# Eight Strassen steps in eight units of a hybrid decoder block, with halves joined and biases added by accumulating transfers

## The chip, the cores and the metric

The kernel runs on one core of a Trainium2 chip. The metric is the device time of one execution in microseconds (us); lower is better. "Before" and "after" name the kernel without and with the change.

## The reference

One layer of a decoder block over 256 tokens of width 4096, in float32. Everything large in it is a product of a 256-row activation with a weight matrix:

```
h      = rmsnorm(x, norm_w)                                # 256 x 4096
proj   = h @ w_in                                          # 4096 x 20480
u_p, z_p, u_c, b_c, c_c, z_c (2048 each), g_logit (8192) = split(proj)
y_pool = (pooled(u_p) @ pool_w, four groups) * pool_scale * silu(z_p)
y_conv = b_c * conv3(c_c * u_c) * silu(z_c)                # causal, width 3
br     = y_pool @ w_branch[0], y_conv @ w_branch[1]        # 2048 x 4096 each
merged = sum over n of sigmoid(g_logit[n] + gate_b[n]) * br[n]
out    = rmsnorm(x + merged @ w_out, final_norm_w)         # 4096 x 4096
```

## The kernel before

**Units and steps.** The work is cut into units of 1024 output columns: for the product with `w_in` the units cu, cc, cz, cb (convolution branch, two of each), pz, pu (pooling branch, two of each) and g0_0 to g1_3 (gates, two branches by four column blocks); for `w_branch` b0_0 to b1_3; for `w_out` o0 to o3. A unit goes through its contraction dimension in steps of 256 rows: 16 steps, in the branch units 8. A step loads one block of 256 x 1024 weights (1 MB) on SyncE's queue into one of three buffers (`raw`).

**Precision by splitting.** An operand is kept as a high part rounded to TensorE's float32r and a low part that holds the rest. Each product is three matmuls: high by high, high by low, low by high. ScalarE makes the high part (line 69), VectorE subtracts to make the low part (line 72). The split weights go into `ring`, a circular store of 60 pieces of 1 KB a partition; preparation runs at most three steps ahead of the multiplication (`AHEAD`) and stops when the ring is full.

**Two kinds of step.** A P step is 2 x 2 x 2 plain block products of 128 x 128 by 128 x 512: 24 matmuls, and two copies and two subtractions of 1024 columns to prepare it; it takes 16 pieces of the ring. An S step is one level of Strassen's scheme (the variant with shared sums): seven block products, 21 matmuls, and in preparation sums of weight blocks as well (`V`, `raw`), with three copies and three subtractions; it takes 28 pieces. For an S step the stationary operand, 128-column blocks of the activation, needs four sums besides its own four blocks (Q3, Q5, Q6, Q7). There is room for these in seven of the 16 operands of a unit (`NS_X = 7`, the operands at 9 to 15); the other nine (`NP_X = 9`) can only be used in P steps. Which steps of a unit are S is written out by the functions `sequence`, `late_sequence` and `spread_sequence` (lines 539 to 572).

**End of a unit.** The products of S steps accumulate in two sets of PSUM banks. One set (`sums`) is evacuated by ScalarE into `E`, the other (`shared`) is joined into `R` (or `Y` in cu1) by `joins`, on ScalarE and VectorE. Then `combine` (line 447) has VectorE add E to R: in one piece of 2048 columns, or in two of 1024 where the unit has `halves` set (gates and outputs). What follows for the unit, its `epi`, is a list of small operations and empty places; `tick` (line 1110) takes one entry for every six matmuls of the next unit. A gate's list is

```python
return gap(1) + halves(lambda t: add(R[:, t], R[:, t], Y[:, 0])) + gap(3) + [
    lambda: act(R, R, AF.Sigmoid), lambda: move(gates_d[n, c], R)]
```

where `Y[:, 0]` holds the bias, loaded three quarters into the unit. An output unit's list loads x into E, adds it to R in two halves after ten empty places, takes the squares on ScalarE, multiplies by the final norm's weights (Y) and stores R (line 753).

**Order.** All instructions are kept in program order on their engine. A transfer written as `move` is issued by GpSimd's queue, `load` by SyncE's. GpSimd runs ahead of the others until something it must wait for holds it, and it then holds whatever stands behind it. From g1_3 on, operands of the branch units, and later of the output units, are fetched from memory by `move` into `sa` (and into `sb` beside it) and filled in by ScalarE and VectorE as their places become free (`pop_fill`, line 838); a fill is put at least six ticks behind its fetch.

**Memory of a partition.** `R`, `E` and `Y` are 8 KB each for the whole kernel. `Y` holds the product of the convolution and pooling branches, from g0_0 on the biases, then the gate that a branch unit needs, and final norm weights.

Of the kernel before, what the change touches and what calls it, by code (L numbers as in the profile page):

```python
# [56 lines left out]
def hybrid_block(ctx: ExitStack, tc: tile.TileContext, x, x_t, norm_t, w_first, w_in, pool_w, pool_scale,  # L57
# [34 lines left out]


# [13 lines left out]
    Y = sb("Y", [P, 2, NU])  # L107
# [19 lines left out]
    m_d = dram.tile([4, P, 4, 2, T], F32, name="m_d")  # L127
    z_d = dram.tile([2, P, 2, NU], F32, name="z_d")
    o_d = dram.tile([3, P, 2, NU], F32, name="o_d")

# [16 lines left out]


    place = {}

    def replace_by(name):
        if place:
            place["stack"].close()
        place["stack"] = stack = ExitStack()
        ctx.enter_context(stack)
        return stack.enter_context(tc.tile_pool(name=name, bufs=1))
# [24 lines left out]
    class Operand:  # L181


        def __init__(self, kind, view, region):
            self.kind, self.view, self.region = kind, view, region
            self.ready = False

# [39 lines left out]
    class Step:  # L227
# [95 lines left out]
        def groups(self):  # L323
# [14 lines left out]
            elif self.kind == "P":  # L338
                order = [(t, n) for n in self.halves for t in self.toks]
                if self.ending:  # L340
                    order = [(t, n) for t in self.toks for n in self.halves]
                for t, n in order:
                    mm = []
                    for k in range(2):
                        ah, al = self.op.standing(k, t)
                        h, l = self.h[n][:, k], self.l[n][:, k]
                        mm += [(ah, h), (ah, l), (al, h)]
                    gs.append([("E", t, n), mm, None])
                    if self.final and t == self.toks[-1]:
                        gs[-1][2] = [(self.blocks[n], 8)]  # L350
            elif self.kind == "S":
                prods = {"M1": (A11, self.dh, self.dl, 0, ("F", 0, 0)),
                         "N3": (Q3, self.dh, self.dl, 1, ("E", 0, 0)),
                         "M2": (A12, self.dh, self.dl, 2, ("E", 0, 1)),
                         "N5": (Q5, self.h13, self.l13, 0, ("F", 0, 1)),
                         "N7": (Q7, self.h13, self.l13, 1, ("F", 1, 0)),
                         "N6": (Q6, self.h24, self.l24, 0, ("F", 1, 1)),
                         "N4": (A22, self.h24, self.l24, 1, ("E", 1, 1))}
                order = ("N3", "M2", "N4", "M1", "N5", "N7", "N6") if self.closing else (
                    "M1", "N3", "M2", "N5", "N7", "N6", "N4")  # L360
                v = self.op.view
                left = {}
                for nm in order:
                    o, h, l, i, bank = prods[nm]
                    mm = [(v[:, 0, o], h[:, i]), (v[:, 0, o], l[:, i]), (v[:, 1, o], h[:, i])]
# [190 lines left out]
    few = NS_X - NB  # L556

# [77 lines left out]
    def make_bands(c):  # L635
        if c == 0:
            pool = replace_by("bands")
            place.update(bands=pool.tile([P, 2, T], F32R, name="bands"), edge=pool.tile([P, 2, P], F32R, name="edge"))
            for t in range(16):
                pin(nc.gpsimd.memset(ic[:, t:t + 1], 1.0 / (t + 1)))  # L640
        bands, edge = place["bands"], place["edge"]
# [21 lines left out]
    def band_sums(st):  # L663
        c = st.band
        for b in range(8):
# [3 lines left out]
            bands, edge = place["bands"], place["edge"]  # L669
# [73 lines left out]
    def out_unit(c):  # L743
# [5 lines left out]
        def epi(u):  # L749
# [3 lines left out]
            return [lambda: move(E, xrows[:, :, cs])] + gap(10) + halves(lambda t: add(R[:, t], R[:, t], E[:, t])) + gap(3) + [  # L753
# [4 lines left out]
        seq = seq_even if c else seq_late  # L758
        if c == 3:

            seq = spread_sequence(NS_X, 1, TAIL)
# [256 lines left out]

    def before(i, fn, *args):
# [156 lines left out]
    def run_step(u, st):  # L1176
# [12 lines left out]
        while not st.op.ready:  # L1189
            pop_fill(True)  # L1190
        gs = st.groups()
# [10 lines left out]
    for u in units:  # L1202
# [4 lines left out]
        if u is last_x:  # L1207
            stages.append(replace_by("more").tile([P, 4, P], F32, name="sb"))
# [3 lines left out]
        for st in u.steps:  # L1212
# [6 lines left out]
            pump()  # L1219
            if u.before and st is u.steps[len(u.steps) * 3 // 4]:  # L1220
# [153 lines left out]
```

## Time and profile before

| | us |
|---|---|
| median of 3 runs | 2393.96 (2393.4 to 2394.25) |
| the profiled execution | 2393.45 |
| its span, first to last instruction | 2391.7 |
| mean granted TensorE clock | 0.999 of full speed |
| VectorE busy | 2101.4 |
| ScalarE busy | 1351.9 |

Times in a profile are us from the start of the span unless marked ns. PE is TensorE's matmul, PEld its load of the stationary operand, DVE is VectorE, ACT ScalarE, POOL GpSimd and SP SyncE. In a group, `out<-in` gives the program's names for what is written and read, then the shape, `xcount`, and behind the bar the busy time, the mean length in ns of one, and behind the next bar how long the engine sat idle just before these instructions and what ended most of that time. In a row of a timeline stand the start, the length, the engine, the line and the instruction, and in brackets the idle time before it. L69 is the helper for ScalarE, L72 the one for two-operand operations of VectorE, L91 that for a transfer of GpSimd's queue, L1122 the matmul of P and S steps.

### The profile page before, as it was taken

Reading aid. Unit: us, or ns where it says so; the run is one execution under the profiler, and the core shown is the slowest. Engines: PE = TensorE matmul, PEld = TensorE weight load, DVE = VectorE, ACT = ScalarE, POOL = GpSimd, SP = SyncE. Lnnn points to the kernel's source line nnn. Section 1 sums busy time; section 2 is a strip of 40 time slices with the busy share of each in tenths; the row PEclk is TensorE's granted clock in tenths of the full one; section 3 lists DMA queues with packets and bytes.
Section 4 is the critical chain, followed back from the end, with each engine's and each line's share of the span. In section 5 each row is a group of like instructions: output and inputs, shape, how many; then the busy total and the mean of one; then the engine's idle time right before and its main releaser. Section 6 shows DMA issues by size and latency. Waiting matters only on the chain.

```text
span 2391.7 us, 27786 instructions
## 1 busy us (share of the span) xinstructions
PE 2379.3 (99%) x10604; PEld 1971.1 (82%) x10604; DVE 2101.4 (88%) x2095; ACT 1351.9 (57%) x1392; POOL 60.6 (3%) x134
## 2 busy tenths in 40 slices
PE   9999999999999999999999999999999999999998
PEld 7888888888888888888888888888888888888886
DVE  8889999888989868968999899889888786799998
ACT  7555555555546555556555556555665555556554
POOL 0000000000000000000000000000000001000000
PEclk9999999999999999999999999999999999999999
DMA  8455565555566455546666556566766668556657
GB/s 335 172 198 198 220 232 208 201 207 194 216 242 229 184 181 224 220 176 221 236 237 229 219 216 225 209 244 236 264 241 234 223 251 290 201 214 247 251 211 273
DMA packets 79942, 538.73 MB, mean 225 GB/s; under 512 B 9280, under 2 KB 9280, under 8 KB 18624
## 3 DMA queue, kind: packets, MB, share of 16 engines
q1 hardware_dynamic: 68384, 484.51, 54.3%
q0 software_dynamic: 10992, 51.39, 6.5%
q8 instruction: 83, 1.36, 0.2%
q10 hardware_dynamic: 432, 1.07, 0.1%
q14 instruction: 51, 0.42, 0.1%
HBM read 511.75 MB, written 25.17 MB: 224 GB/s over the span
## 4 chain that ended last, share of the span: by engine, by line
PE 99%; DVE 0%; DMA 0%; ACT 0%; issue 0%; DVEq 0%; SPq 0%; ACTq 0%
PE sums L1122 79%; PE shared L1122 19%; PE shared L691 1%; PE shared L467 1%; DMA R<-in_x_t_dram 0%; PE shared L670 0%; PE shared L671 0%; PE shared L673 0%; PE shared L672 0%; DVE raw L1308 0%; DVE E L84 0%; ACT V L69 0%; ACT arena L69 0%; DVE raw L1304 0%; PE shared L972 0%
## 5 line engine op out<-in xcount | busy, mean ns | idle before, releaser
L1122 PE MATMUL sums<-ring,arena 128*128 128x512 f32 x8292 | 1941.7, 390 | 0.3 <-ACT arena L69 0.3
L1122 PEld LDWEIGHTS sums<-ring,arena 128*128 128x128 f32 x8292 | 1554.5, 188 | 322.5 <-ACT ring L69 1.2
L69 ACT ACTIVATE ring<-raw 128x1024 fp32r<-128x1024 f32 (+2 forms) x901 | 988.5, 1136 | 736.3 <-PE sums L1122 264.0
L72 DVE TENSOR_TENSOR ring<-raw,ring 128x1024 fp32r<-128x1024 f32 (+2 forms) x901 | 1162.0, 1321 | 216.3 <-ACT ring L69 184.2
L1122 PE MATMUL shared<-ring,arena 128*128 128x512 f32 x1968 | 497.2, 389 | 0.0
L1122 PEld LDWEIGHTS shared<-ring,arena 128*128 128x128 f32 x1968 | 369.4, 188 | 76.6
L69 ACT ACTIVATE ring<-V 128x1024 fp32r<-128x1024 f32 x164 | 173.2, 1056 | 109.4 <-DVE V L72 75.3
L72 DVE TENSOR_TENSOR V<-raw 128x1024 f32<-128x1024 f32 x164 | 199.7, 1217 | 0.6 <-DMA raw<-in_w_out_dram 0.5
L72 DVE TENSOR_TENSOR ring<-V,ring 128x1024 fp32r<-128x1024 f32 x164 | 199.8, 1218 | 0.3 <-ACT ring L69 0.2
L72 DVE TENSOR_TENSOR raw<-raw 128x512 f32<-128x512 f32 x164 | 113.5, 692 | 5.7
L72 DVE TENSOR_TENSOR raw<-V,raw 128x512 f32<-128x512 f32 x164 | 113.3, 691 | 5.0
L72 DVE TENSOR_TENSOR R<-R,E 128x1024 f32<-128x1024 f32 (+1 forms) x55 | 95.0, 1744 | 1.9 <-DMA E<-gates_d 1.0
L69 ACT ACTIVATE E<-sums,rin 128x512 f32<-128x512 f32 (+1 forms) x57 | 44.8, 828 | 34.9 <-PE sums L1122 34.6
L72 DVE TENSOR_TENSOR R<-R,shared 128x512 f32<-128x512 f32 x84 | 57.3, 682 | 1.1
L69 ACT ACTIVATE arena<-sa 128x512 fp32r<-128x512 f32 (+2 forms) x45 | 24.9, 572 | 53.9 <-DVE sa L72 49.0
L72 DVE TENSOR_TENSOR R<-R,Y 128x1024 f32<-128x1024 f32 (+1 forms) x28 | 40.3, 1446 | 0.0
L72 DVE TENSOR_TENSOR arena<-sa,arena 128x512 fp32r<-128x512 f32 (+2 forms) x45 | 27.2, 621 | 11.7 <-ACT arena L69 11.7
L69 ACT ACTIVATE R<-R 128x2048 f32<-128x2048 f32 x8 | 15.3, 1911 | 14.5 <-DVE R L72 14.5
L467 PEld LDWEIGHTS shared<-ident,R 128*128 128x128 f32 x160 | 19.4, 140 | 4.2
L467 PE MATMUL shared<-ident,R 128*128 128x128 f32 x160 | 22.6, 272 | 0.0
L691 PE MATMUL shared<-ring 128*128 128x512 f32 x96 | 22.1, 389 | 0.0
L691 PEld LDWEIGHTS shared<-ring 128*128 128x128 f32 x96 | 18.0, 188 | 3.7
(131 smaller groups left out, 395.4 us busy)
## 6 DMA issues: line engine op xcount, KB each, us to landing
raw<-in_w_in_dram SPq DMA_DIRECT2D x319, 1024.0 KB, 4.9
raw<-in_w_branch_dram SPq DMA_DIRECT2D x64, 1024.0 KB, 5.7
raw<-in_w_out_dram SPq DMA_DIRECT2D x64, 1024.0 KB, 5.0
gates_d<-R POOLq DMA_DIRECT2D x8, 1024.0 KB, 5.3
raw<-in_pool_w_dram SPq DMA_DIRECT2D x4, 1024.0 KB, 4.7
Y<-in_gate_b_dram POOLq DMA_DIRECT2D x8, 512.0 KB, 6.5
Y<-gates_d POOLq DMA_DIRECT2D x4, 1024.0 KB, 10.0
E<-gates_d POOLq DMA_DIRECT2D x4, 1024.0 KB, 5.6
```

The costliest lines, as they stand in the source:

```text
L69: return pin(nc.scalar.activation(dst, src, func, **kw))
L72: return pin(nc.vector.tensor_tensor(out=dst, in0=a, in1=b, op=op))
L467: pin(nc.tensor.transpose(shared(j)[:, i * T + t * P:i * T + (t + 1) * P], src[:, t, c:c + P], ident))
L691: pin(nc.tensor.matmul(o, a[:, k, ts], b[:, k], start=(k, i) == (0, 0), stop=(k, i) == (3, 2)))
L1122: pin(nc.tensor.matmul(ps, lhs, rhs, start=n == 0, stop=n == u.total[b] - 1))
```

## The change

Four things change together.

1. A new helper issues a transfer on GpSimd's queue that adds its source to its destination. In cu1, cz, pz, all gate units, b0 and o0 to o2, `combine` uses it to add E to R (E to Y in cu1), and nine empty places follow. The bias of a gate is added in the same way, from the bias in memory, read once for each partition and token half; so is x in o0 to o2.
2. Y is thereby no longer used from the end of pu1's work in g0_0 until the branch units. Its place is given to four sums and one block of operand 8 (`LATE`), which so can be used in an S step: these are formed in cc0 (`late_sums`), stored, read back and split in g0_0, and likewise in o1 for the output units, where Y shrinks to half.
3. Six gate units (all but g0_0 and g1_3) and o2 and o3 take eight S steps where they had seven.
4. By the table `SPREAD`, pu0 and cz1 take seven S steps, spread, where they had six at the end.

```diff
+    def move_add(dst, src):
+        return pin(nc.gpsimd.dma_start(dst, src, accum_op=ALU.add))
...
         if u.s:
             if not u.flags.get("joined"):
                 join(u)
-            if u.halves:
+            if u.name.startswith(('cu1', 'cz', 'pz', 'g', 'b0', 'o0', 'o1', 'o2')):
+
+                queue.append(lambda: move_add(d, E))
+                queue.extend(gap(9))
+            elif u.halves:
                 queue.extend(halves(lambda t: add(d[:, t], d[:, t], E[:, t])))
...
+    SPREAD = {"pu0":(7,),"cz1":(7,5)}
...
+        if name in SPREAD:
+            seq = spread_sequence(*SPREAD[name])
...
-            move(Y[:, 0], gate_b[0, n, None, c * NU:(c + 1) * NU].to_broadcast([P, NU]))
-
         def epi(u):
-            return gap(1) + halves(lambda t: add(R[:, t], R[:, t], Y[:, 0])) + gap(3) + [
+            bias = gate_b[0, n, None, None, c * NU:(c + 1) * NU].to_broadcast([P, 2, NU])
+            return [lambda: move_add(R, bias)] + gap(9) + [
                 lambda: act(R, R, AF.Sigmoid), lambda: move(gates_d[n, c], R)]
 
         seq = {(0, 0): seq_late, (1, 3): spread_sequence(few)}.get((n, c), seq_even)
+        if (n, c) in ((1, 0), (0, 1), (1, 1), (0, 2), (1, 2), (0, 3),):
+            seq = spread_sequence(NS_X + 1, 1 if c else 2)
...
-            return [lambda: move(E, xrows[:, :, cs])] + gap(10) + halves(lambda t: add(R[:, t], R[:, t], E[:, t])) + gap(3) + [
+            return [lambda: move_add(R, xrows[:, :, cs])] + gap(9) + [
                 square] + halves(lambda t: mul(R[:, t], R[:, t], Y[:, 0])) + [lambda: move(o_d[c], R)]
...
+        if c in (2, 3,):
+            seq = spread_sequence(NS_X + 1)
         if c == 3:
 
-            seq = spread_sequence(NS_X, 1, TAIL)
+            seq = spread_sequence(NS_X + 1, 1, TAIL)
...
+    LATE = NP_X - 1
+
+    def late_sums():
+        o = x_ops[LATE]
+        h, l = (o.view[:, part].bitcast(F32) for part in range(2))
+        q = sa[:, 4:8].rearrange("p (k t) c -> p k t c", t=2)
+        add(q, h, l)
+        q = q.rearrange("p k t c -> p k (t c)")
+        mul(q, q, rbc[:, None].to_broadcast([P, 2, T]))
+        sums_s(sa, [sa[:, i] for i in range(4, 8)])
+        mul(sa[:, Q3], sa[:, Q3], std)
+        move(late_d[:, 0:4], sa[:, 0:4])
+        move(late_d[:, 4], sa[:, A11])
...
+    def late_split(o, q, src):
+        act(q[:, 0], src)
+        sub(q[:, 1], src, q[:, 0].bitcast(F32))
+        o.more_ready = True
+
+    def late_m():
+        nonlocal Y
+        pool = replace_by("late_m", lower)
+        stages.pop()
+        Y = pool.tile([P, 1, NU], F32, name="Y")
+        sums_s(sa, [sa[:, i] for i in range(4, 8)])
+        late_split(m_ops[LATE], late_place(pool, m_ops[LATE], (Q3, Q5, Q6, Q7)), sa[:, 0:4])
...
+    before(23, late_sums)
...
+            if u.name == "g0_0" and st is u.steps[2]:
+                move(sa[:, 0:5], late_d)
+            if u.name == "g0_0" and st is u.steps[8]:
+                queue.append(lambda: late_split(x_ops[LATE], late_place(
+                    replace_by("late", lower), x_ops[LATE], (Q3, Q5, Q6, Q7, A11)), sa[:, 0:5]))
+            if u.name == "o1" and st is u.steps[6]:
+                assert not fills
+                move(flat(sa[:, 4:8]), m_d[LATE // 4][:, LATE % 4].rearrange("p k t -> p (k t)"))
+                queue.extend(gap(7) + [late_m])
```

`late_place` only allots the place, and `Operand.block` looks a block up in its old or its new place. The rest of the diff takes Y out of the fixed memory and makes the places that follow one another there.

More of the change, by code (lines that the diff above doesn't have):

```diff
@@ L127, in hybrid_block, with close, replace_by @@
     m_d = dram.tile([4, P, 4, 2, T], F32, name="m_d")
+    late_d = dram.tile([P, 5, P], F32, name="late_d")
     z_d = dram.tile([2, P, 2, NU], F32, name="z_d")
     o_d = dram.tile([3, P, 2, NU], F32, name="o_d")
+    lower, upper = {}, {}
+    def close(place):
+        if place:
+            place["stack"].close()
+            place.clear()
+    def replace_by(name, place=upper):
+        close(upper)
+        close(place)
+        place["stack"] = stack = ExitStack()
+        ctx.enter_context(stack)
+        return stack.enter_context(tc.tile_pool(name=name, bufs=1))
+    Y = replace_by("y", lower).tile([P, 2, NU], F32, name="Y")
     xrows = xf.rearrange("(t p) d -> p t d", p=P)
@@ L186, in __init__, with block @@
             self.ready = False
+            self.more = None
+            self.more_ready = False
+        def block(self, part, i):
+            if self.kind == "S":
+                return self.view[:, part, i]
+            if i in self.more:
+                return self.more[i][:, part]
+            return self.view[:, part, {A12: 0, A22: 0, A11: 1, A21: 1}[i], i in (A22, A21)]
     busy = {}
@@ L360, in groups @@
                     "M1", "N3", "M2", "N5", "N7", "N6", "N4")
-                v = self.op.view
+                v = self.op.block
                 left = {}
@@ L668, in band_sums @@
             cs = slice(b * P, (b + 1) * P)
[L669 removed]
+            bands, edge = upper["bands"], upper["edge"]
             pin(nc.tensor.matmul(o, st.h[:, 0, cs], bands[:, g], start=True, stop=False))
@@ L1017, in x_parts, with late_place @@
             sub(o.view[:, 1, a:b], sa[:, a:b], o.view[:, 0, a:b].bitcast(F32))
+    LATE = NP_X - 1
[10 more added lines that the diff above has]
+        move(late_d[:, 4], sa[:, A11])
+    def late_place(pool, o, blocks):
+        n = len(blocks)
+        q = pool.tile([P, 2, n, P], F32R, name="sums")
+        o.more = {b: q[:, :, i] for i, b in enumerate(blocks)}
+        return q
+    def late_split(o, q, src):
[9 more added lines that the diff above has]
+        late_split(m_ops[LATE], late_place(pool, m_ops[LATE], (Q3, Q5, Q6, Q7)), sa[:, 0:4])
     def before(i, fn, *args):
@@ L1190, in run_step @@
             pop_fill(True)
+        assert st.kind != "S" or st.op.kind == "S" or st.op.more_ready
         gs = st.groups()
@@ L1207, in hybrid_block @@
         if u is last_x:
+            Y = replace_by("y_b", lower).tile([P, 2, NU], F32, name="Y")
             stages.append(replace_by("more").tile([P, 4, P], F32, name="sb"))
```

14 lines of the change are left out of this document (3 added, 11 removed).

## The prediction

> **What bounds the kernel now.** I read the page's first part, then its chain of work that ended last, then the same chain in order of time.
>
> ```profile
> span 2391.7 us, 27786 instructions
> PE 2379.3 (99%) x10604; PEld 1971.1 (82%) x10604; DVE 2101.4 (88%) x2095; ACT 1351.9 (57%) x1392; POOL 60.6 (3%) x134
> PE 99%; DVE 0%; DMA 0%; ACT 0%; issue 0%; DVEq 0%; SPq 0%; ACTq 0%
> L1122 PE MATMUL sums<-ring,arena 128*128 128x512 f32 x8292 | 1941.7, 390 | 0.3 <-ACT arena L69 0.3
> L1122 PE MATMUL shared<-ring,arena 128*128 128x512 f32 x1968 | 497.2, 389 | 0.0
> ```
>
> The chain that sets the end is TensorE for 99% of it, and the two groups of large matmuls sat idle 0.3 us in all. A busy engine is not yet one at its peak, so the rate comes next: the chain's rows give a start, a length and a count.
>
> ```profile
> 2318.24 6.12 PE sums L1122 x27
> 2363.80 17.01 PE sums L1122 x75
> 2380.84 0.43 DVE R L72
> ```
>
> 6.12 / 27 = 0.2267 us and 17.01 / 75 = 0.2268 us for a matmul of 512 columns. The two groups hold 8292 + 1968 = 10260 of them, 10260 x 0.2267 = 2326 us of the 2391.7; the rest is transposes, the pooling matmuls, the start and the 11 us after 2380.84, in which the result is finished. So the time is a count of matmuls times a constant. A step of plain products (P) issues 24 and a Strassen step (S) 21; the count fits 284 P and 164 S.
>
> What holds the number of S steps down is VectorE. By form:
>
> ```profile
> L72 DVE TENSOR_TENSOR ring<-raw,ring 128x1024 fp32r<-128x1024 f32 x731 | 863.9, 1221 | 139.6 <-ACT ring L69 107.7 <-PE sums L1122 21.3 <-issue 0.6
> L72 DVE TENSOR_TENSOR ring<-raw,ring 128x1536 fp32r<-128x1536 f32 x164 | 287.7, 1754 | 71.0 <-ACT ring L69 70.8
> L72 DVE TENSOR_TENSOR V<-raw 128x1024 f32<-128x1024 f32 x164 | 199.7, 1217 | 0.6 <-DMA raw<-in_w_out_dram 0.5
> L72 DVE TENSOR_TENSOR R<-R,E 128x2048 f32<-128x2048 f32 x27 | 61.8, 2289 | 1.8 <-DMA E<-gates_d 1.0
> L72 DVE TENSOR_TENSOR R<-R,E 128x1024 f32<-128x1024 f32 x28 | 33.2, 1217 | 0.1
> L72 DVE TENSOR_TENSOR R<-R,Y 128x1024 f32<-128x1024 f32 x22 | 26.6, 1217 | 0.0
> ```
>
> Rows overlap a little, so I take a pair from starts, in the timeline of VectorE in g1_0, with TensorE's beside it:
>
> ```profile
> 1144.45 1.22 DVE L72 TENSOR_TENSOR V<-raw 128x1024 f32<-128x1024 f32 x1
> 1146.32 1.75 DVE L72 TENSOR_TENSOR ring<-raw,ring 128x1536 fp32r<-128x1536 f32 x1
> 1149.98 3.50 DVE L72 TENSOR_TENSOR ring<-raw,ring 128x1024 fp32r<-128x1024 f32 x3
> 1153.39 1.22 DVE L72 TENSOR_TENSOR V<-raw 128x1024 f32<-128x1024 f32 x1
> ```
> ```profile
> 1148.07 0.87 PE L1122 MATMUL shared<-ring,arena 128*128 128x512 f32 x3
> 1158.33 0.84 PE L1122 MATMUL shared<-ring,arena 128*128 128x512 f32 x3
> ```
>
> One S and one P take VectorE 1153.39 - 1144.45 = 8.94 us, of which P has two of the last three rows, 2.27, and S 6.67. TensorE takes 45 x 0.2267 = 10.20 us for the pair. So a pair wins VectorE 1.26 us, an S behind an S loses 6.67 - 4.76 = 1.91 us, and exchanging a P for an S costs it 4.40 us. The same rows show the smallest margin: the 128x1536 subtraction ended at 1148.07 and the first product that reads it began at 1148.07. Here VectorE has nothing left. Elsewhere it has more, as windows of one unit each show (columns: stretch, length, busy PE, PEld, DVE, ACT, POOL, clock, DMA share, GB/s):
>
> ```profile
> 1127.00:1209.00 82.00, 82.00 (x363) 67.90 (x362) 79.52 (x74) 48.62 (x47) 1.07 (x2) 1.00 0.66 246
> 1209.00:1291.00 82.00, 82.00 (x364) 67.92 (x363) 73.88 (x69) 46.74 (x44) 1.05 (x2) 1.00 0.60 224
> 2134.00:2216.00 82.00, 82.00 (x363) 67.90 (x362) 77.96 (x74) 47.69 (x48) 1.79 (x3) 1.00 0.66 249
> ```
>
> They are g1_0, g0_1 and o1.
>
> **The change, part by part.** *Matmuls.* Six gate units and o2, o3 go from seven S to eight; the new table of spread sequences also takes pu0 and cz1 from six to seven, which the change's title does not say. That is ten P turned into S, 30 matmuls fewer: 30 x 0.2267 = **6.80 us**, all on the chain as long as TensorE is never made to wait.
>
> *VectorE.* Added: 10 x 4.40 = 44.0 us, and the sums for the eighth pair, by these rows:
>
> ```profile
> L72 DVE TENSOR_TENSOR sa<-sa 128x128 f32<-128x128 f32 x36 | 8.9, 288 | 0.5
> L72 DVE TENSOR_TENSOR arena<-sa,arena 128x512 fp32r<-128x512 f32 x37 | 25.3, 687 | 11.7 <-ACT arena L69 11.7
> ```
>
> In cc0 two ops of 512 columns and five of 128 (2.8 us), in g0_0 one subtraction of 640 (0.8, an estimate between the 512 and the 1024 rows), in o1 four of 128 and one of 512 (1.9): 5.5 us. Removed: all 28 R<-R,E of 128x1024 (8 gate units and three output units join in halves, and three outputs add x: 16 + 6 + 6), 34.1 us; 16 of the 22 R<-R,Y (the biases), 19.5 us; seven of the 27 of 128x2048 (cz, pz, b0), 16.0 us; one like them into Y, 2.3 us. That is 71.9 us out and 49.5 in. In a gate unit 4.40 come in and four adds of (3.50 - 1.22) / 2 = 1.14 from start to start go, 4.56: 73.9 - 0.2 = 73.7 us of VectorE in a unit that now lasts 360 x 0.2267 = 81.6. Its share stays at nine tenths; the lead that the preparation of operands has over TensorE does not shrink on the mean. ScalarE copies three pieces instead of two for a new S; at 46.7 of 82 us in g0_1 it has room.
>
> *Local lead.* The new order in a gate unit is P S P S P S P S S P S P S P S P (g1_0 has two such doubles), in cz1 three S stand in a row, and o3 has three doubles. A double costs 1.91 us of lead, a triple 3.8. In g0_1 the lead is larger than that:
>
> ```profile
> 1231.50 1.76 DVE L72 TENSOR_TENSOR ring<-raw,ring 128x1536 fp32r<-128x1536 f32 x1 [0.68 <-ACT ring L69]
> 1240.61 0.84 PE L1122 MATMUL shared<-ring,arena 128*128 128x512 f32 x3
> ```
>
> Ready at 1233.26, read at 1240.61: 7.35 us. In g1_0 the tight point at 1148 gets the four adds ahead of it back (4.5 us) and pays the small subtraction in g0_0, net about 3.7 us of lead; its two doubles, with pairs between them, draw about 2.1 of that. In o1 the four adds go as well, against 1.9 us of new sums. I cost local lead at nothing. If I am wrong by all of it the price is 2 us at a double.
>
> *Accumulating transfers.* There are 30, of 1 MB each: 19 joins, 8 biases, 3 of x. They go out on GpSimd's queue, and nothing in the trace is such a transfer. The issue of a plain one on that queue, and rows near it with the KB of each and the median us from issue to landing (the last two rows are the queues' packets, MB and share of 16 engines):
>
> ```profile
> L91 POOL DMA_DIRECT2D gates_d<-R x8 | 4.3, 536 | 468.3 <-ACT R L69 391.8 <-DVE raw L72 76.5
> ```
> ```profile
> gates_d<-R POOLq DMA_DIRECT2D x8, 1024.0 KB, 5.3
> Y<-in_gate_b_dram POOLq DMA_DIRECT2D x8, 512.0 KB, 6.5
> Y<-gates_d POOLq DMA_DIRECT2D x4, 1024.0 KB, 10.0
> q0 software_dynamic: 10992, 51.39, 6.5%
> q1 hardware_dynamic: 68384, 484.51, 54.3%
> ```
>
> An accumulate must read both its operands. Bounds for a join: 5.3 us (it costs no more than a plain copy) to 10.6 (two copies one behind the other; the slowest 1 MB row is 10.0). For a bias, whose source is one row read for all partitions: 6.5 to 2 x 6.5 + 5.3 = 18.3. I take 10.6 and 13.0, two reads each, since nothing excludes the second read. Below nothing is excluded: a transfer takes time. The Trainium skill ("Collectives: The Full Stack", The bandwidth ceiling) says that a reducing DMA has two source reads on the same read ring and measured it 1.93 times slower than a copy; by that a join would be an estimated 10.2 us. No run here shows it yet.
>
> Who waits for them? In g0_1, from the timelines of ScalarE and VectorE:
>
> ```profile
> 1208.77 1.45 ACT L69 ACTIVATE E<-sums,rin 128x512 f32<-128x512 f32 x2
> 1222.24 1.90 ACT L69 ACTIVATE R<-R 128x2048 f32<-128x2048 f32 x1
> ```
> ```profile
> 1211.39 0.68 DVE L72 TENSOR_TENSOR R<-R,shared 128x512 f32<-128x512 f32 x1
> ```
>
> The second row is the sigmoid. It stood ninth in the list of the unit's closing work, of which an entry is taken every six matmuls: 9 x 6 x 0.2267 = 12.2 us into the next unit; it began 13.5 us after the last evacuation. Now it stands twenty-first: 28.6 us. The last write of the join ends at 1212.07 and leaves R ready 3.3 us into the unit. Two accumulates in series with 0.54 us of issue each: 3.3 + 0.54 + 10.6 + 0.54 + 13.0 = 28.0 us, just in time. At both low ends it is 16.2, at both high ends 33.3, 4.7 us late, which the 7.35 us of lead covers in g0_1. For cz and pz one transfer stands ahead of the sigmoid at entry 15 (20.4 us), for b0 ahead of a multiply at 13 (17.7 us). Those are met by 10.6. So I cost them at nothing; the cover is the lead.
>
> *What queues behind the waits.* GpSimd issues in order. The second accumulate waits there for the first to land, and behind it stand the fetches of the next operands and the stores of R. That such a wait holds the queue is seen already:
>
> ```profile
> POOL Y L91 <- DMA m_d<-Y: 5.1, 2, 4.4
> ```
>
> The Trainium skill ("DMA: Bandwidth & Descriptors", Rules for kernel authors) says that an accumulate reads its destination and writes later, with nothing holding the bytes between, so the earlier transfer's semaphore must be waited for. By it the two cannot overlap, which the sum above already has.
>
> The tightest fetch is the first in g1_3 (timeline of ScalarE):
>
> ```profile
> 1620.59 1.25 ACT L69 ACTIVATE E<-sums,rin 128x512 f32<-128x512 f32 x2
> 1627.11 0.61 ACT L69 ACTIVATE arena<-sa 128x512 fp32r<-128x512 f32 x1
> 1631.86 1.92 ACT L69 ACTIVATE R<-R 128x2048 f32<-128x2048 f32 x1 [4.14 <-DVE R L72]
> ```
>
> The middle row is the fill. Its fetch now follows g0_3's join on the queue, issued 3.3 us after 1620.6, and lands behind it at about 1620.6 + 3.3 + 0.5 + 10.6 = 1635, so ScalarE would stand some 8 us at that fill. But it stood 4.14 us for the sigmoid's input there and spent 1.9 on it, and both move later: about 2 us net, out of the lead. Without any lead there it would be 2 us.
>
> *Transfers and loads.* 30 MB more, read twice, over a queue that took 6.5% of the span for 51.39 MB adds about 2 x 31.5 / 51.39 x 6.5 = 8 points to a share of 60.8 (54.3 + 6.5). Weight loads have three buffers; one delayed by an accumulate's engine time (2 x 3.2 us) is late by a microsecond or two and draws on the same lead.
>
> *Sum.* The profiled execution took 2393.45 us, 1.75 more than its span: 2393.45 - 6.80 = 2386.65. The median of the runs stands 0.51 above it: 2393.96 - 6.80 = **2387.2 us**, 0.28% less.
>
> **Rivals.** (a) *Small waits.* Margins now at zero (g1_0, o1) are not won back, doubles of S or late fetches make TensorE wait 1 to 2 us at two to four places: 2 to 6 us back, 2389 to 2393. For it: the zero margin at 1148 and VectorE at 79.5 of 82 us. Against: VectorE loses 22 us of work in all.
>
> (b) *Slow accumulates.* With T each, the sigmoid is late by 3.3 + 2 x (0.54 + T) - 28.6 = 2T - 24.2 us; ScalarE stands there and prepares nothing behind it. TensorE stops when that exceeds 7.35, so from T = 15.8 us. At T = 20, nearly four plain transfers, 8.4 us in each of 8 gate units and 3 output units (whose squares stand at entry 21 too): 93 us, 2480. At 17 us it is 2.4 x 11 = 27 us, 2414. For it: broadcast reads are slow (6.5 us for half a MB), and loads hold half the engines. Against: the stores at 5.3 us land beside those same loads.
>
> (c) *It does not do what it says.* If the joins stayed behind VectorE's work, or fewer steps changed, TensorE's count would not fall; the count is set by the sequences, so I give this nothing of its own.
>
> (d) *Loads fall behind.* If accumulates take the DMA engines for much longer than two reads, weights come late everywhere: a stall of 1 us at each of 30 gives 2417. It goes with (b).
>
> **How the numbers follow.** Forecast (TensorE unbroken, losses under 2 us) 0.64; (a) 0.20, of which three quarters within 0.2%; (b) and (d) 0.16, nearly all slower. A difference of 0.2%, 4.8 us, is about what a measurement of this kernel can tell from none. Faster by more needs under 2389.2: 0.64 and a little of (a), 0.65; within it 0.18; slower 0.17. The range goes from 2385.5 (run to run about half a us, a stall or two of before gone) over (a) to 2396, where the least cases of (b) begin; the likeliest case alone is 2386 to 2389.
>
> **What would show it.** Right: 10230 large matmuls still at 0.2267 us, idle before them still under a microsecond, R<-R,E halves gone, accumulates landing in 9 to 13 us, and the sigmoid waiting on nothing or on a transfer for under 5 us. Wrong: a row of TensorE waiting for ring data in the hundreds of ns many times over (a), or ScalarE's R rows waiting for DMA by more than 7 us in each gate unit (b). A landing time above 15.8 us would make the prediction wrong by itself.

## The result and the profile after

The change made the kernel slower. The median of 14 runs is 2400.10 us (2396.13 to 2402.89), beside 2393.98 us (2393.40 to 2396.28) for 14 runs of before; the ratio is 1.0022, with a 95% interval of 1.0014 to 1.0031. The forecast was 2387.2 us, and the range ended at 2396. Also new is the spread: 6.8 us between the runs after, 2.9 before. It goes with TensorE's mean granted clock, which is 0.998 in the two fastest runs after (2396.13 and 2396.28 us) and 0.996 in the slowest (2402.89).

The page of the profiled execution after (2400.57 us) begins so; the last lines are rows of its fifth and sixth part.

```profile
span 2398.9 us, 27805 instructions
PE 2379.2 (99%) x10574; PEld 1967.4 (82%) x10574; DVE 2082.1 (87%) x2096; ACT 1366.4 (57%) x1404; POOL 88.3 (4%) x157
L1188 PE MATMUL sums<-ring,arena 128*128 128x512 f32 x8118 | 1911.5, 390 | 7.5 <-ACT E L69 5.5
L1188 PE MATMUL shared<-ring,arena 128*128 128x512 f32 x1998 | 505.6, 389 | 0.1
R<-E POOLq DMA_DIRECT2D x18, 1024.0 KB, 9.6
R<-in_gate_b_dram POOLq DMA_DIRECT2D x8, 1024.0 KB, 11.4
R<-in_x_dram POOLq DMA_DIRECT2D x3, 1024.0 KB, 13.0
q0 software_dynamic: 15024, 76.42, 12.4%
```

TensorE has its 30 matmuls less (10574 for 10604), and the span is 7.2 us longer all the same: 7.2 + 6.8 = 14.0 us have been lost on the way. The busy time hides it: 99% as before. What tells is the third column of the two groups, idle 7.5 us where it was 0.3, and the engine named for 5.5 of them: **ScalarE writing E**, that is an evacuation of PSUM, and not operands in the ring. VectorE did get its relief (2101.4 to 2082.1 us), and the accumulates land in 9.6 to 13.0 us at the median.

Where TensorE stood is found in its timeline: three places. These are the ends of g1_0 and of o1 and the middle of g1_3 (start, length, then what ran; in brackets the idle time).

```profile
1201.18 6.28 PE L1188 MATMUL sums<-ring,arena 128*128 128x512 f32 x27
1209.76 7.34 PE L1188 MATMUL sums<-ring,arena 128*128 128x512 f32 x24 [2.31 <-ACT E L69]
...
1672.66 0.49 PE L1188 MATMUL sums<-ring,arena 128*128 128x512 f32 x1 [0.61 <-ACT ring L69]
1673.92 5.51 PE L1188 MATMUL sums<-ring,arena 128*128 128x512 f32 x23 [0.77 <-DVE ring L72]
...
2211.80 6.28 PE L1188 MATMUL sums<-ring,arena 128*128 128x512 f32 x27
2221.28 8.62 PE L1188 MATMUL sums<-ring,arena 128*128 128x512 f32 x24 [3.20 <-ACT E L69]
```

Look at the lengths, not only at the brackets. 24 matmuls took 7.34 us at 1209.76 and 8.62 us at 2221.28; 24 at the usual rate take 24 x 0.2267 + 0.17 = 5.61. So 1.7 and 3.0 us more were lost behind the waits, on matmuls that ran slowly. The windows around them show why (the column of 0.79 and 0.72 is the granted clock of TensorE; elsewhere it is 1.00):

```profile
1208.00:1216.00 8.00, 6.24 (x20) 5.00 (x21) 7.87 (x10) 4.76 (x7) 0.85 (x1) 0.79 0.49 147
2218.00:2230.00 12.00, 8.80 (x27) 6.90 (x27) 9.60 (x11) 6.01 (x8) 0.87 (x1) 0.72 0.57 171
```

0.21 of 8 us is 1.7, 0.28 of 12 us is 3.4: after each of the two waits the clock was halved for a while. (In o1 the half clock began at 2220.64, 0.6 us before TensorE went on, so not all of the 3.4 us was lost on matmuls.) From the last start before a wait to the first behind it, less one matmul, g1_0's end cost 1209.76 - (1201.18 + 26 x 0.2267) - 0.23 = 2.5 us, o1's end 3.4, and the two waits near 1672 1.8 together (1.0 + 1.26 us between starts). With the slow matmuls: 2.5 + 1.7 + 3.4 + 3.0 + 1.8 = 12.4 of the 14.0 us. A further 0.7 us is in 114 matmuls that read the eighth operand's new place (below); 0.9 us is not placed.

**Why ScalarE was late.** In g1_0, from the timelines of GpSimd and ScalarE:

```profile
1136.95 0.90 POOL L94 DMA_DIRECT2D R<-E  x1 [59.54 <-PE sums L1188]
1146.08 1.22 POOL L94 DMA_DIRECT2D R<-in_gate_b_dram  x1 [8.23 <-DMA R<-E]
```
```profile
1122.50 2.25 ACT L69 ACTIVATE E<-sums,rin 128x1024 f32<-128x1024 f32 x3
1132.29 0.58 ACT L69 ACTIVATE R<-shared 128x512 f32<-128x512 f32 x1
1158.89 1.92 ACT L69 ACTIVATE R<-R 128x2048 f32<-128x2048 f32 x1 [4.24 <-DMA R<-in_gate_b_dram]
```

g1_0's first matmul is at 1125.56, so the first accumulate is issued 11.4 us into the unit, not 3.3: the join of g0_0 only begins at 1132.29, behind preparation on ScalarE and VectorE. g0_0 ends in an S step, so its shared banks close with its last matmul and the join falls into the next unit; g0_1, where I had read the 3.3 us, follows a unit that ends in a P step and whose join had begun before its end. The sigmoid then stands 4.24 us for the bias, and with it all preparation. o0 ends in an S step too, and its squares stood in o1 for x (GpSimd's issue, then ScalarE):

```profile
2145.06 0.87 POOL L94 DMA_DIRECT2D R<-E  x1 [53.67 <-DVE R L72]
```
```profile
2167.05 1.06 ACT L69 ACTIVATE E<-R 128x1024 f32<-128x1024 f32 x1 [4.97 <-DMA R<-in_x_dram]
```

In g1_3 it is a fetch behind g0_3's accumulate (GpSimd, then ScalarE at the fill):

```profile
1623.18 0.85 POOL L94 DMA_DIRECT2D R<-E  x1 [53.37 <-DVE R L72]
1623.72 0.89 POOL L91 DMA_DIRECT2D sa<-y_d  x1
```
```profile
1636.74 0.63 ACT L69 ACTIVATE arena<-sa 128x512 fp32r<-128x512 f32 x1 [9.78 <-DMA sa<-y_d]
```

**From a late ScalarE to a waiting TensorE.** At the end of g1_0, ScalarE's timeline again:

```profile
1202.71 1.49 ACT L69 ACTIVATE ring<-raw 128x1536 fp32r<-128x1536 f32 x1 [2.50 <-DMA raw<-in_w_in_dram]
1204.11 1.04 ACT L69 ACTIVATE ring<-V 128x1024 fp32r<-128x1024 f32 x1
1207.16 1.06 ACT L69 ACTIVATE ring<-raw 128x1024 fp32r<-128x1024 f32 x1 [2.01 <-DVE raw L72]
1208.12 0.58 ACT L69 ACTIVATE R<-shared 128x512 f32<-128x512 f32 x1
1208.60 1.11 ACT L69 ACTIVATE E<-sums,rin 128x1024 f32<-128x1024 f32 x1
```

The last row empties the banks that g0_1's first matmul writes. It stands in program order behind the preparation of g0_1's S step at step 1, whose weights came late and which VectorE had yet to sum. That load took the usual 4.9 us; it was issued only at 1197.71, when VectorE had freed its buffer. With the lead gone, that preparation reaches ScalarE when the evacuation is due. So far this is an argument from order; e5 and e7 try it.

### The profile page after: what moved, and what is told of

The parts are those of the page before. It is cut to its first block, busy times and chain, and to the rows that moved or that the text cites. A ratio compares the mean times of both kernels' runs of the same rounds, so it can differ in the third digit from the quotient of the medians.

```text
span 2398.9 us, 27805 instructions
## 1 busy us (share of the span) xinstructions
PE 2379.2 (99%) x10574; PEld 1967.4 (82%) x10574; DVE 2082.1 (87%) x2096; ACT 1366.4 (57%) x1404; POOL 88.3 (4%) x157
## 3 DMA queue, kind: packets, MB, share of 16 engines
q0 software_dynamic: 15024, 76.42, 12.4%
## 5 line engine op out<-in xcount | busy, mean ns | idle before, releaser
L1188 PE MATMUL sums<-ring,arena 128*128 128x512 f32 x8118 | 1911.5, 390 | 7.5 <-ACT E L69 5.5
L1188 PEld LDWEIGHTS sums<-ring,arena 128*128 128x128 f32 x8118 | 1524.0, 188 | 326.6 <-ACT E L69 6.3
L1188 PE MATMUL shared<-ring,arena 128*128 128x512 f32 x1998 | 505.6, 389 | 0.1
L69 ACT ACTIVATE ring<-V 128x1024 fp32r<-128x1024 f32 x174 | 183.9, 1057 | 121.0 <-DVE V L72 79.0
L72 DVE TENSOR_TENSOR V<-raw 128x1024 f32<-128x1024 f32 x174 | 212.1, 1219 | 4.0 <-DMA raw<-in_w_in_dram 2.4
L72 DVE TENSOR_TENSOR ring<-V,ring 128x1024 fp32r<-128x1024 f32 x174 | 212.0, 1218 | 3.0 <-ACT ring L69 3.0
L72 DVE TENSOR_TENSOR raw<-V,raw 128x512 f32<-128x512 f32 x174 | 120.3, 691 | 5.5
L94 POOL DMA_DIRECT2D R<-E x18 | 15.7, 870 | 913.1 <-DVE R L72 624.7
L72 DVE TENSOR_TENSOR R<-R,E 128x2048 f32<-128x2048 f32 x20 | 45.8, 2289 | 0.8 <-DMA E<-gates_d 0.2
L1188 PE MATMUL shared<-ring,sums 128*128 128x512 f32 x90 | 23.3, 395 | 0.0
## 6 DMA issues: line engine op xcount, KB each, us to landing
R<-in_gate_b_dram POOLq DMA_DIRECT2D x8, 1024.0 KB, 11.4
```

The source lines that it names most:

```text
L69: return pin(nc.scalar.activation(dst, src, func, **kw))
L72: return pin(nc.vector.tensor_tensor(out=dst, in0=a, in1=b, op=op))
L94: return pin(nc.gpsimd.dma_start(dst, src, accum_op=ALU.add))
L1188: pin(nc.tensor.matmul(ps, lhs, rhs, start=n == 0, stop=n == u.total[b] - 1))
```

## The experiments

The theory tried, called W in the expectations: ScalarE's waits for late accumulates and fetches use up the lead, the eight S steps keep it from coming back, and at a unit's end TensorE pays for it, with a half clock on top. Rivals: D, the doubles of S steps are too much for VectorE whatever the transfers do; C, the accumulates take DMA engines from the weight loads everywhere. All times below are medians; kernels of one group ran beside the same runs of before. Those had 2394.30 us for e1 to e4, 2394.05 for e5 to e8 and 2393.95 for e9 and e10.

**e1: accumulates without the extra S steps.**

```diff
-    SPREAD = {"pu0":(7,),"cz1":(7,5)}
+    SPREAD = {}
-        if (n, c) in ((1, 0), (0, 1), (1, 1), (0, 2), (1, 2), (0, 3),):
+        if (n, c) in ():
-        if c in (2, 3,):
+        if c in ():
-            seq = spread_sequence(NS_X + 1, 1, TAIL)
+            seq = spread_sequence(NS_X, 1, TAIL)
```

> The changed kernel with the sequences of before (164 S steps, 10260 large matmuls); accumulates, their gaps and the late operand's sums stay. Theory W (ScalarE standing for late accumulates in g1_0 and o1, 4.2 and 5.0 us, and for a late fetch in g1_3, 9.8 us, uses up the lead; eight S steps then keep it from coming back until a unit's end, where TensorE waits for an evacuation that stands behind preparation on ScalarE and loses its clock): the three ScalarE waits stay at 4 to 10 us each, but with seven S the lead comes back, TensorE waits under 1.5 us in all and 2393 to 2396 us. Rival D (the doubles of S alone are too much for VectorE, the accumulates are harmless): TensorE waits for nothing, 2393 to 2394.5, and ScalarE's waits are of no account. Rival C (accumulates cost by taking DMA engines from the weight loads everywhere): 2397 or more, with many waits for weights.

Measured 2396.12 us, ratio 1.0008 (0.9999 to 1.0018). The waits of ScalarE for transfers are nearly all there:

```profile
ACT arena L69 <- DMA sa<-y_d: 14.6, 2, 8.7
ACT E L69 <- DMA R<-in_x_dram: 6.6, 2, 3.4
ACT R L69 <- DMA R<-in_gate_b_dram: 3.4, 1, 3.4
```

but TensorE stood for ring and arena 1.6 us in all, no evacuation held it and its clock stayed whole. With seven S steps the lead comes back. It is what W gives, a little over its 2396 and its 1.5 us; rivals D (no waits of account) and C (2397 or more) both miss. But this edit also moves S steps at the boundaries: with seven, the first S of g0_1 and of o2 stands at step 2 and not at step 1. o1 itself has seven S steps in both kernels, so at its end it is the place that differs. e5 takes count and place apart.

**e2: the extra S steps without accumulates.**

```diff
-            if u.name.startswith(('cu1', 'cz', 'pz', 'g', 'b0', 'o0', 'o1', 'o2')):
+            if u.name.startswith('none'):
-            return [lambda: move_add(R, bias)] + gap(9) + [
+            return [lambda: move(E, bias)] + gap(9) + halves(lambda t: add(R[:, t], R[:, t], E[:, t])) + gap(3) + [
-            return [lambda: move_add(R, xrows[:, :, cs])] + gap(9) + [
+            return [lambda: move(E, xrows[:, :, cs])] + gap(8) + halves(lambda t: add(R[:, t], R[:, t], E[:, t])) + gap(2) + [
```

> The changed kernel's 174 S steps, but all joins on VectorE again, and biases and x loaded into E by a plain transfer and added there by VectorE: no accumulating transfer is left. Theory W: the ScalarE waits for accumulates go, but VectorE has 4.4 us more in each unit of eight S (78 of 81.6 us), g1_0 where before had no margin falls behind by about 4 us; TensorE waits 2 to 6 us there and in o3, and with half clock behind it 2390 to 2398. Rival D: the same doubles and more VectorE work, so stalls in every gate unit, above 2400. Rival C: the loads recover, under 2389.

Measured 2404.46 us, ratio 1.0042 (1.0027 to 1.0057), worse than W had it (2390 to 2398). The windows of g1_0 and o1 show VectorE at its end in g1_0, 83.21 of 85 us, and at 81.83 of 87 us in o1:

```profile
1127.00:1212.00 85.00, 82.27 (x360) 66.99 (x358) 83.21 (x78) 48.62 (x45) 1.30 (x2) 1.00 0.64 232
2136.00:2223.00 87.00, 82.97 (x363) 67.53 (x361) 81.83 (x80) 47.83 (x49) 2.33 (x4) 1.00 0.62 234
```

and TensorE stood at the same two unit ends, 5.7 us for E, with the half clock behind both, and 4.4 us for operands. So the accumulates earn their place: without them the S steps cost 4.4 us more than with them. D's number came (above 2400), though not its stalls in every gate unit, and its part is real: in g1_0 there is no room for eight S steps if VectorE joins. In o1 it is seven S steps and the sums for the eighth operand. The way TensorE is stopped does not ask who used up the lead.

**e3: later readers.**

```diff
-            return [lambda: move_add(R, bias)] + gap(9) + [
+            return [lambda: move_add(R, bias)] + gap(13) + [
-            return [lambda: move_add(R, xrows[:, :, cs])] + gap(9) + [
+            return [lambda: move_add(R, xrows[:, :, cs])] + gap(9 if c == 2 else 14) + [
```

> The changed kernel with the sigmoid of a gate put 4 entries later (13 empty places behind the bias instead of 9) and the squares of o0 and o1 5 later (14 for 9); 5.4 and 6.8 us. Theory W: ScalarE no longer stands for R in g1_0 and o1 (under 0.5 us), the two waits of TensorE at the ends of g1_0 and o1 go with their half clock (4.0 and 6.5 us in the profile), what is left is g1_3 with 1.8 us: 2388 to 2391. Rival D: the lead is drained by doubles all the same, both waits stay at more than half: 2396 to 2401. Rival C: no change, 2398 to 2401.

Measured 2391.67 us, ratio 0.9990 (0.9980 to 0.9999): 8.4 us less than the change for a few empty places. ScalarE has no wait for a bias or for x left, and both long waits of TensorE are gone, one of them to

```profile
1208.89 5.45 PE L1188 MATMUL sums<-ring,arena 128*128 128x512 f32 x22 [0.83 <-ACT E L69]
```

0.83 us at the end of g1_0 with the full clock behind it (1.00 from 1206 to 1218). W held, 0.7 us over its range; a bit of its gain was spent in b1_0, where TensorE waited 1.5 us and the store of g1_3's gates, now later too, held the next join (ScalarE stood 4.3 us for it).

**e4: later fills.**

```diff
         if u is last_x:
+            LANDING = 12
...
             units_done[0] = True
+            LANDING = 6
```

> The changed kernel with fills placed at least 12 ticks behind their fetch in g1_3 instead of 6 (8.2 us more). Theory W: ScalarE's wait of 9.8 us at the first fill of g1_3 falls under 3 us, TensorE's two waits near 1672 go (1.8 us), and g1_0 and o1 stay as they are: 2396 to 2399.5, and less spread between runs. Rival D and rival C: the waits near 1672 stay, 2398 to 2401.

Measured 2398.27 us, ratio 1.0016 (1.0007 to 1.0025). ScalarE's wait at the first fill of g1_3 is gone, and with it TensorE's waits near 1672, as W had it. The time alone would not tell, since 2398.27 lies in the rivals' range too; it is 1.8 us less, as those waits cost, but a new wait of 1.3 us in o1 is in the trace as well. The 8.4 us that ScalarE still stands at a fill are in b0_0, at 1721, and were there in the change too (8.5); there the lead bears them. The spread hardly shrank (2395.44 to 2401.53).

**e5: a P step behind the boundary.**

```diff
-            seq = spread_sequence(NS_X + 1, 1 if c else 2)
+            seq = spread_sequence(NS_X + 1, 1 if (c, n) > (1, 0) else 2)
-            seq = spread_sequence(NS_X + 1)
+            seq = spread_sequence(NS_X + 1, 2)
```

> The changed kernel with the first S of g0_1 and of o2 at step 2 instead of step 1 (still eight S each). Theory W, its last part (TensorE waits at the end of g1_0 and o1 because the evacuation stands on ScalarE behind the preparation of an S step one ahead, late for want of its weights): with a P step in that place both waits fall under 1.7 us and no half clock follows, 2390 to 2394; ScalarE's waits for R in g1_0 and o1 stay at 4 to 5 us. Rival: the lead alone decides, not what stands ahead of the evacuation: the waits stay over 2 us, 2398 to 2401.

Measured 2396.56 us, ratio 1.0010 (1.0001 to 1.0019), between the two expectations. At the end of g1_0 and o1 the waits did fall, to about 0.8 and 0.4 us from matmul to matmul and without a half clock, though ScalarE stood 4.3 and 4.8 us for the bias and x (4.2 and 5.0 in the change). Behind g1_0 nothing more was paid: at the next boundary where an S step is at step 1, g0_1 to g1_1, TensorE does not wait. Behind o1 it was: at the end of o2, which has eight S steps, TensorE waited 2.8 us for E and lost its clock (0.86 of 12 us). e1, with seven there and the same place of the first S in o3, has no such wait. So what stands ahead of an evacuation decides where a lost lead is paid, and at g1_0 whether it is.

**e7: the two late units alone.**

```diff
-            return [lambda: move_add(R, bias)] + gap(9) + [
+            return [lambda: move_add(R, bias)] + gap(9 if n or c else 13) + [
-            return [lambda: move_add(R, xrows[:, :, cs])] + gap(9) + [
+            return [lambda: move_add(R, xrows[:, :, cs])] + gap(9 if c else 14) + [
```

> The changed kernel with the longer empty places behind g0_0's bias (13) and o0's x (14) and nothing else; all other units keep 9. Theory W: these two units alone, whose join is late because their last step is an S step, carry the loss: ScalarE's waits for R go, TensorE's two long waits and the half clock go, g1_3's two waits near 1672 stay (2 us): 2389 to 2392, and the waits that the run with later readers had in b1_0 are not there. Rival: other units' sigmoids matter too: 2394 or more.

Measured 2392.33 us, ratio 0.9994 (0.9985 to 1.0003), 0.3 over the expected range. Two units out of eleven, g0_0 and o0, carry 7.8 us of the loss. There the join is late; in the other nine units nine empty places are enough (ScalarE stands 0.2 us for biases in all). The wait of 4.3 us for the gates' store is gone, as expected, though one of 1.3 us for E has come at the start of b1_0.

**e6: all three edits** (those of e4, e5 and e7 together).

> The changed kernel with all three edits: four more empty places behind g0_0's bias and five behind o0's x (those two units alone), fills of g1_3 at least 12 ticks behind their fetch, and the first S of g0_1 and o2 at step 2. Theory W: every wait of TensorE for ScalarE is gone, 30 matmuls of 0.2267 us are saved and the 114 with the new operand cost 0.7 us: 2387 to 2389, under both kernels. Rival: something else of the change still costs, 2390 or more.

Measured 2388.91 us (2387.83 to 2389.70), ratio 0.9977 (0.9969 to 0.9986): under both kernels. The page's first line, and TensorE's whole list of waits (their sum, count and longest):

```profile
span 2386.4 us, 27812 instructions
```
```profile
PE shared L959 <- DVE rout L964: 1.1, 1, 1.1
PE sums L1188 <- ACT ring L69: 0.4, 1, 0.4
PE sums L1188 <- ACT arena L69: 0.4, 1, 0.4
PE sums L1188 <- ACT E L69: 0.2, 1, 0.2
```

1.1 us is at the start, as before; the rest is 1.0 us. ScalarE still stands 8.4 us at a fill and 2.9 for a bias, and with the lead kept that costs TensorE no more than this. The span is 5.3 us shorter than before's 2391.7 where 30 matmuls make 6.8: 1.0 of waits and 0.7 of slower matmuls with the new operand make up about the difference. 11.2 of the 12.9 us between the forecast and the change have been found.

**e9: the same without the later S step.** The edits of e4 and e7.

> The kernel with all three edits less the third: the first S of g0_1 and o2 is at step 1 again; the longer chains of g0_0 and o0 and the later fills of g1_3 stay. Theory W: with the lead kept, the evacuation ahead of an S step's preparation is late by about 1 us at the end of g1_0 (1.2 us from matmul to matmul in the run with the longer chains only), g1_3 has no wait and no half clock comes: 2389 to 2391. Rival (the place of the first S is what matters): 2393 or more.

Measured 2390.54 us, ratio 0.9985 (0.9976 to 0.9994); ScalarE's E held TensorE 0.9 us in two places. As W had it: with the lead kept, the place of the first S is worth 1.6 us (2390.54 - 2388.91).

**e10: e9 with the sequences of before** (the edits of e1, e4 and e7).

> The longer chains and later fills with the sequences of before (10260 large matmuls, 164 S steps): accumulating transfers without the ten new S steps, and without the waits. Theory W: the accumulates are free once nobody stands for them, and win nothing by themselves, since TensorE is the bound: 2393.5 to 2395, so the ten S steps are worth 5 to 6.5 us against the kernel with all three edits. Rival (the accumulates free VectorE and win by that): 2392 or less. Rival C (they cost by taking DMA engines from the loads): 2396 or more.

Measured 2395.40 us, ratio 1.0005 (0.9996 to 1.0015), a little over the expected 2395. TensorE waits for nothing but at the start. So the accumulates win nothing by themselves, and rival C is out as the cause: of the 447 weight loads, 63 were in flight beside an accumulate for over 2 us and took 8.3 us at the median, the 374 that met none 5.0, and no wait of TensorE came of it. The ten S steps are worth 2395.40 - 2390.54 = 4.9 us against e9, which differs by them alone, and 6.5 us against e6, which has one edit more. The 1.4 us over before lie within the interval; in the trace they are at the start and in the finish behind the last matmul. Whether the transfers of x make that finish later was not tried.

**e8: waits set in the kernel before.**

```diff
         if t == 0:
+            for _ in range({"g0_1": 5, "g1_1": 6, "g0_2": 7, "g1_2": 8, "g0_3": 6}.get(u.name, 0)):
+                act(E[:, 0], E[:, 0])
             act(dst[:, t], PE0.rearrange("p n c -> p (n c)"), **kw)
```

> The kernel before, in which ScalarE copies E onto itself (128x1024, 1.05 us each) ahead of the evacuation of the first half: 5 times at the end of g0_1, 6 of g1_1, 7 of g0_2, 8 of g1_2, 6 of g0_3; E is dead there, the output stays the same. It sets waits of TensorE of about 0.5 to 4 us. Theory W (a wait of 2.3 us or more costs a half clock on top, one of 1.7 us or less does not): matmuls at 0.427 us in a row, 8 or 16 of them, behind the longer waits only. Rival (the half clock had to do with the accumulating transfers or the eight S steps): none here, since neither is in this kernel.

One execution, 2411.80 us. Five waits came of it, and the clock answered one (TensorE's timeline, then the windows):

```profile
1294.77 3.41 PE L1124 MATMUL sums<-ring,arena 128*128 128x512 f32 x13 [2.60 <-ACT E L69]
...
1465.22 1.66 PE L1124 MATMUL sums<-ring,arena 128*128 128x512 f32 x6 [2.80 <-ACT E L69]
...
1552.28 10.05 PE L1124 MATMUL sums<-ring,arena 128*128 128x512 f32 x36 [3.89 <-ACT E L69]
```
```profile
1292.00:1304.00 12.00, 9.40 (x41) 7.42 (x41) 8.73 (x10) 7.82 (x9) 0.00 (x0) 1.00 0.23 87
1463.00:1475.00 12.00, 9.49 (x40) 7.54 (x41) 8.39 (x8) 8.69 (x9) 0.00 (x0) 1.00 0.00 1
1550.00:1562.00 12.00, 9.72 (x36) 7.78 (x37) 8.34 (x8) 8.72 (x9) 0.00 (x0) 0.86 0.01 1
```

Behind 3.89 us the clock halved (0.86 of 12 us, and 36 matmuls in 10.05 us instead of 8.3), behind 2.60, 2.80 and two waits of 1.71 it did not, while in the changed kernel 2.31 us was enough. So the half clock needs neither accumulates nor S steps: that rival is out. But the limit that I had set at 2.3 us fell with it: 2.60 and 2.80 us lie above it, and 2.26 us, which was enough in e4, below. The Trainium skill ("TensorE: Matmul & The Clock Gate", What's actually happening) says that the clock is halved after an idle window of about 3.4 us, and that these windows run freely and do not start anew with the kernel. The traces agree on the windows and not on the idle: 2.31 us is no whole window, and there the measurement decides.

The traces give the condition more closely. Windows of 1 us show where the two half clocks of the change begin, at 1210.30 (half for 0.70 of 1 us) and at 2220.64 (0.36):

```profile
1210.00:1211.00 1.00, 1.00 (x4) 0.80 (x4) 0.96 (x3) 1.00 (x2) 0.00 (x0) 0.65 0.58 66
2220.00:2221.00 1.00, 0.00 (x0) 0.00 (x0) 1.00 (x1) 1.00 (x2) 0.00 (x0) 0.82 0.00 0
```

They last 3.41 and 6.83 us, and their starts are 1010.34 us apart, 296 steps of 3.4133 us; in e2 and e4 the two starts lie as far apart. So in these runs the clock changes in steps of 3.413 us that the waits do not move. In e8 the half clock begins at 1552.96. Counted back from there, a step ends at 1293.55, within the wait of 2.60 us, and one at 1464.21, within that of 2.80, so that neither wait leaves more than 1.8 us of idle in one step. The 2.31 us of the change lie whole in the step that ends at 1210.30. In all the traces, behind the start, a half clock begins after each of the eight steps with 2.26 to 2.88 us of idle and after no step with 1.79 us or less. Between the two nothing was measured. It lasts one step, and two in o1 of the change, where TensorE still idled 0.6 us of the first.

## Why the prediction was wrong

- **The saving was right.** 30 matmuls at 0.2267 us, ten S steps: 6.8 us forecast, 4.9 by e10 against e9. e9's waits of TensorE (1.2 us) and the 0.7 us of slower matmuls are of the size of the rest.
- **VectorE was nearly right.** 22.4 us less were forecast and 19.3 measured.
- **The accumulates' time was right.** 9.6 us for a join (10.6 taken) and 11.4 for a bias (13.0). The Trainium skill ("Collectives: The Full Stack", The bandwidth ceiling) has two reads and a ratio of 1.93; the trace agrees with the ratio, 9.6 to the 5.3 of a plain store being 1.8, and does not show the reads. The sum counted the issue twice, 0.54 us each: these times run from the start of the issue. The threshold of 15.8 us for slow accumulates was not reached, and that rival did not come.
- **The step that failed first** is "the last write of the join ... leaves R ready 3.3 us into the unit". It was read in g0_1 and used for every unit. The rows of before held the answer: g0_0 and o0 end in an S step and cannot be joined sooner. These two, TensorE's first of g1_0 and VectorE's last of the join, are from the trace of before:

```profile
1126.99 3.34 PE L1122 MATMUL sums<-ring,arena 128*128 128x512 f32 x14
1136.91 0.69 DVE L72 TENSOR_TENSOR R<-R,shared 128x512 f32<-128x512 f32 x1
```

  There R is ready 10.6 us into the unit. With 11.4, as measured after, in place of 3.3, the sum in g1_0 is 11.4 + 9.1 (from the first issue to the second) + 12.8 (this bias; the median is 11.4) = 33.3 us against an entry at 28.6. ScalarE got there 0.5 us late and stood 4.24. The transfer times were there; the start of the chain was not. The prediction's own sign of being right, a sigmoid that waits under 5 us, let this through; the other, matmuls idle for under a microsecond, did not (7.5).
- **"I cost local lead at nothing"** then failed where it was weakest. g1_0 did win back its lead at first, as argued (the subtraction that ended at 1148.07, with no margin, now ends at 1142.09, 4.7 us ahead of its product), but 4.24 us of wait and two doubles used it. The sums for lead and for waits had been made apart, each with the same 7.35 us of cover, which was g0_1's.
- **The late fetch** was foreseen and mis-sized for ScalarE: "some 8 us at that fill", "about 2 us net", was 9.78 us. The sigmoid that it was to replace came later in the same unit, at 1657, and its 1.9 us still had to be paid there. What TensorE lost by it, 1.8 us, is near the 2 us named for the case without lead.
- **Weight loads beside an accumulate** were to be late "by a microsecond or two". They took 8.0 us at the median and up to 11.3, against 4.9 for the loads that met none; by e10 this alone costs no time.
- **The price of a wait was missing.** The rival that came true is the one of small waits, at 2 to 6 us back; it was 14. I had only asked whether operands in the ring are ready in time. TensorE was held by an evacuation behind other work on ScalarE, and each long wait took the clock with it: 2.5 and 3.4 us of wait cost 4.2 and 6.4. With a gain of 6.8 us, two such waits decide the sign.

What stays open: where between 1.79 and 2.26 us of idle in a step the half clock sets in, why matmuls with the new operand run slower, and 0.9 of the 14.0 us.

## What to carry to other kernels

A gain of 0.3% on an engine that is 99% busy is lost by two waits, so the chain ahead of each reader is to be followed in the unit where it starts latest, and not in a typical one. Where an engine works in order, ask what stands ahead of the instruction that frees a bank, and put a reader of a slow transfer where the slowest chain is met: here nine more empty places in two lists took back 7.8 us, more than the whole gain of the 30 matmuls. A wait of TensorE of over 2 us can bring a stretch of half clock, here 1.7 or 3.0 us more, and is to be priced with it; whether it comes depends on how the wait lies to the clock's steps.

## What the runs showed of the hardware

- Half clock: matmuls 0.427 us apart instead of 0.227, for 3.41 or 6.83 us. It came behind waits of 2.26 and 3.21 (e4), 2.31 and 3.20 (the change), 2.34 and 3.40 (e2), 2.83 (e5) and 3.89 us (e8), and not behind 2.60 and 2.80 us (e8). What told was the idle time in one step of 3.413 us: 2.26 us or more, against 1.79 or less.
- A matmul whose stationary operand lies in the eighth operand's new place takes 395 ns where the others take 390, and the next follows it after 0.233 us instead of 0.227: 114 of them, 0.7 us.

```profile
L1188 PE MATMUL shared<-ring,sums 128*128 128x512 f32 x90 | 23.3, 395 | 0.0
L1188 PE MATMUL sums<-ring,sums 128*128 128x512 f32 x24 | 6.9, 395 | 0.0
```

- An accumulating transfer of 1 MB from SBUF to SBUF landed in 9.6 us beside the weight loads, one whose source is a row of memory read for all partitions in 11.4, one that adds rows of x in 13.0. In the change 59 of the 447 weight loads were in flight beside one for over 2 us and took 8.0 us at the median, up to 11.3; the 364 that met none took 4.9, as before (4.9).
